# Rotary embedding on half of each head: first tile loaded in two pieces, tables from GpSimd, stores and loads regrouped

## The chip, the cores and the metric

The kernel runs on one core of one Trainium2 chip; the other cores are idle. The metric is the device time of one execution in microseconds (us). Most executions of one kernel agree within 0.3%.

## The reference

```python
batch, seq, heads, dim = (16, 512, 16, 64)          # x: float32, 33.55 MB
half_dim = dim // 2
x1, x2 = x[..., :half_dim], x[..., half_dim:]
rotated_first  = x1[..., :half_dim//2] * cos - x1[..., half_dim//2:] * sin
rotated_second = x1[..., :half_dim//2] * sin + x1[..., half_dim//2:] * cos
return concatenate([rotated_first, rotated_second, x2], axis=-1)
```

Only the first 32 values of each head's 64 are rotated; the other 32 pass through. `cos` and `sin` (512 x 32; only columns 0 to 15 are used) depend on the position alone. Every byte of `x` has to be read and every byte of the output written: 67.1 MB in all.

## The kernel before

`x` is cut into T = 4 tiles of 128 partitions x K = 16 positions ("rows"). A row is 16 heads x 64 values, 4 KiB, so that a tile is 64 KiB per partition, 8.39 MB. The kernel keeps three tiles (`NS = 3`) in SBUF, the on-chip memory that the transfers fill and empty, so tile 3 reuses tile 0's place and can be loaded only when tile 0 has been stored. VectorE rotates in place in half tiles (`KC = 8` rows), with four instructions each. All transfers are issued from one queue, that of SP, and in the trace their packets run in program order.

```python
def load(t, lo=0, hi=K):
    nc.sync.dma_start(out=rows(t, lo, hi), in_=xf[t, :, lo * R : hi * R])
def store(t, lo=0, hi=K):
    nc.sync.dma_start(out=of[t, :, lo * R : hi * R], in_=rows(t, lo, hi))

load(0)
nc.sync.dma_start(out=stage[:, 0]..., in_=cosf)      # 64 KB each
nc.sync.dma_start(out=stage[:, 1]..., in_=sinf)
load(1)
load(2)
... # 4 copies spread the tables over 128 partitions
def rotate(t, k0):
    ...
    nc.vector.tensor_mul(out=b_t[:], in0=x1, in1=s)  # b_t lies in PSUM
    nc.vector.tensor_mul(out=x1, in0=x1, in1=c)
    nc.vector.tensor_sub(...)
    nc.vector.tensor_add(...)

rotate(0, 0)
store(0, 0, KC)
rotate(0, KC)
store(0, KC, K)
load(3, 0, KC)
load(3, KC, K)
for t in range(1, T):
    rotate(t, 0)
    rotate(t, KC)
    store(t)
```

Of the kernel before, what the change touches and what calls it, by code (L numbers as in the profile page):

```python
# [1 line left out]

# [4 lines left out]


@with_exitstack
def kernel(  # L10
    ctx: ExitStack,
    tc: tile.TileContext,
    x: bass.AP,
    cos: bass.AP,
    sin: bass.AP,
    out: bass.AP,
):
    nc = tc.nc
    fp32 = mybir.dt.float32
    P = 128  # L20
    B, S, H, D = x.shape
    Q = D // 4
    HF = D // 2



    K = 16
    T = B * S // (P * K)
    PB = S // K
    REP = P // PB  # L30
    R = H * D
    NS = 3
    KC = K // 2

    xf = x.rearrange("b s h d -> (b s h d)").rearrange("(t p f) -> t p f", t=T, p=P)
    of = out.rearrange("b s h d -> (b s h d)").rearrange("(t p f) -> t p f", t=T, p=P)
    cosf = cos.rearrange("(p k) j -> p (k j)", k=K)
    sinf = sin.rearrange("(p k) j -> p (k j)", k=K)

    const_pool = ctx.enter_context(tc.tile_pool(name="const", bufs=1))  # L40
    b_pool = ctx.enter_context(tc.tile_pool(name="bp", bufs=1, space=bass.MemoryType.PSUM))


    ring = const_pool.tile([P, NS, K, H, D], fp32)
    stage = const_pool.tile([PB, 2, K, HF], fp32)
    table = const_pool.tile([P, 2, K, 2, Q], fp32)

    def rows(t, lo, hi):
        return ring[:, t % NS, lo:hi].rearrange("p k h d -> p (k h d)")

    def load(t, lo=0, hi=K):
        nc.sync.dma_start(out=rows(t, lo, hi), in_=xf[t, :, lo * R : hi * R])  # L52

    def store(t, lo=0, hi=K):
        nc.sync.dma_start(out=of[t, :, lo * R : hi * R], in_=rows(t, lo, hi))

    load(0)
    nc.sync.dma_start(out=stage[:, 0].rearrange("p k j -> p (k j)"), in_=cosf)  # L58
    nc.sync.dma_start(out=stage[:, 1].rearrange("p k j -> p (k j)"), in_=sinf)
    load(1)  # L60
    load(2)


    for r in range(REP):
        nc.vector.tensor_copy(  # L65
            out=table[r * PB : (r + 1) * PB].rearrange("p t k c j -> p (t k) c j"),
            in_=stage.rearrange("p t k j -> p (t k) j")[:, :, 0:Q]
            .unsqueeze(2)
            .to_broadcast((PB, 2 * K, 2, Q)),
        )  # L70
    C = table[:, 0].rearrange("p k c j -> p k (c j)")
    Sn = table[:, 1].rearrange("p k c j -> p k (c j)")

    def rotate(t, k0):
        x1 = ring[:, t % NS, k0 : k0 + KC, :, 0:HF]
        c = C[:, k0 : k0 + KC].unsqueeze(2).to_broadcast((P, KC, H, HF))
        s = Sn[:, k0 : k0 + KC].unsqueeze(2).to_broadcast((P, KC, H, HF))
        b_t = b_pool.tile([P, KC, H, HF], fp32)
        nc.vector.tensor_mul(out=b_t[:], in0=x1, in1=s)  # L79
        nc.vector.tensor_mul(out=x1, in0=x1, in1=c)  # L80
        nc.vector.tensor_sub(  # L81
            out=x1[:, :, :, 0:Q], in0=x1[:, :, :, 0:Q], in1=b_t[:, :, :, Q:HF]
        )
        nc.vector.tensor_add(  # L84
            out=x1[:, :, :, Q:HF], in0=x1[:, :, :, Q:HF], in1=b_t[:, :, :, 0:Q]
        )

    rotate(0, 0)
    store(0, 0, KC)
    rotate(0, KC)  # L90
    store(0, KC, K)
    load(3, 0, KC)
    load(3, KC, K)
    for t in range(1, T):
        rotate(t, 0)
        rotate(t, KC)
        store(t)


# [1 line left out]
_INS = ['x', 'cos', 'sin']  # L101
_OUTS = [((16, 512, 16, 64), 'float32')]


# [23 lines left out]
```

## Time and profile before

| | before |
|---|---|
| time, median of 3 runs | 162.21 us (162.02 to 162.35) |
| span of the profiled execution | 160.2 us |
| share of 16 DMA engines | 98.0% |
| VectorE busy | 109.5 us, 68% |
| VectorE's first instruction, end of its last | 23.9 us, 134.2 us |

The page of the profile, cut to the lines used. In part 2 each column is a fortieth of the span, about 4 us, and a digit is the busy share in tenths. Part 3 has packets, MB, and the share of 16 engines' time.

```profile
span 160.2 us, 103 instructions
## 1 busy us (share of the span) xinstructions
DVE 109.5 (68%) x36; POOL 0.2 (0%) x4
...
DVE  0000009999999999999999999999999995000000
...
GB/s 262 524 262 524 524 295 524 262 524 507 278 524 475 311 524 327 458 393 434 483 393 401 483 425 393 524 524 262 524 507 278 524 507 278 524 491 295 524 491 33
...
q1 hardware_dynamic: 1536, 67.24, 98.0%
...
DVE 61%; DMA 14%; issue 6%; DVEq 1%; SPq 0%
```

The reader should set two lines against each other. The chain that ended last (the bottom line) gives VectorE 61% and so looks like a kernel bound by VectorE. But the queue is busy 98.0% of the span. The chain follows the releaser of each *instruction*: the last store was issued when VectorE had finished, so the chain runs along VectorE. That the store then stood in a queue of other stores, this view doesn't say. The DVE row shows VectorE idle at the end, while the GB/s row goes on. (The GB/s figures swing because a 64 KiB packet is counted whole in one slice; the mean of neighbours counts.)

The timeline shows the queue of SP directly (start, duration of the issues merged, engine):

```profile
23.88 2.77 DVE L65 COPY table<-stage 32x1024 f32<-32x1024 f32 x4 [23.88 <-DMA stage<-in_sin_dram]
...
40.13 13.79 SPq L55 DMA_DIRECT2D out_dram<-ring  x2
...
72.04 10.44 SPq L52 DMA_DIRECT2D ring<-in_x_dram  x2
...
82.59 51.98 SPq L55 DMA_DIRECT2D out_dram<-ring  x3
...
131.93 2.28 DVE L84 TENSOR_TENSOR ring<-ring,b_t 128x2048 f32<-128x2048 f32 x1
```

Beside these views, the argument uses the trace's packet records (start, duration and size of each transfer on an engine). A 64 KiB packet takes 2.418 us whether it loads or stores. A completion packet of 4 bytes ends each transfer on each engine, so those packets show when the engines finished a transfer. The records don't name the engine: where this text says "per engine", a sum over all 16 is divided by 16. This gives, for three of before's five stores, when each was issued and when the first engine had nothing else to do; the difference is called the margin:

| store | issued at | engines free from | margin |
|---|---|---|---|
| tile 0, first half | 40.1 | 61.4 | 21.3 us |
| tile 2 | 107.4 | 119.6 | 12.2 us |
| tile 3, the last | 134.2 | 138.9 | 4.6 us |

The smallest margin is 4.6 us; the two stores left out have 17 us and more. While such packets run, 16 engines at 65,536 B in 2.418 us move 434 GB/s.

### The profile page before, as it was taken

The page shows a single profiled execution, that of the slowest core. Times are in us where ns is not written, and L with a number is a line of the kernel's source. Part 1 is how long each engine was busy: PE and PEld are TensorE (multiplying, and loading weights), DVE is VectorE, ACT ScalarE, POOL GpSimd, SP SyncE. Part 2 cuts the span into 40 slices and gives each one's busy share as a digit, 9 for nine tenths or more (in the row PEclk, how much of TensorE's full clock was granted, in tenths as well). Part 3 has the DMA queues.
Part 4 walks back from the last instruction along what each step waited for, and adds up shares of the span by engine and source line. Part 5 has one row for each costly group of instructions (what it writes and reads, how often), then busy time and mean ns, then how long its engine had stood idle before and what let it go on. Part 6 is the DMA issues. An engine that isn't in the chain of part 4 may idle for free.

```text
span 160.2 us, 103 instructions
## 1 busy us (share of the span) xinstructions
DVE 109.5 (68%) x36; POOL 0.2 (0%) x4
## 2 busy tenths in 40 slices
DVE  0000009999999999999999999999999995000000
POOL 0000000000000000000000000000000000000000
DMA  8969989699699797999999999996996996996990
GB/s 262 524 262 524 524 295 524 262 524 507 278 524 475 311 524 327 458 393 434 483 393 401 483 425 393 524 524 262 524 507 278 524 507 278 524 491 295 524 491 33
DMA packets 1536, 67.24 MB, mean 420 GB/s; under 512 B 192, under 2 KB 192, under 8 KB 256
## 3 DMA queue, kind: packets, MB, share of 16 engines
q1 hardware_dynamic: 1536, 67.24, 98.0%
HBM read 33.69 MB, written 33.55 MB: 420 GB/s over the span
## 4 chain that ended last, share of the span: by engine, by line
DVE 61%; DMA 14%; issue 6%; DVEq 1%; SPq 0%
DVE b_t L79 22%; DVE ring L80 22%; DMA stage<-in_sin_dram 14%; DVE ring L84 10%; DVE ring L81 6%; DVE table L65 1%; DVEq L123 1%; SPq L58 0%; SPq L52 0%; DVEq L65 0%
## 5 line engine op out<-in xcount | busy, mean ns | idle before, releaser
L79 DVE TENSOR_TENSOR b_t<-ring,table 128x4096 f32<-128x4096 f32 x8 | 35.5, 4432 | 0.3
L80 DVE TENSOR_TENSOR ring<-ring,table 128x4096 f32<-128x4096 f32 x8 | 35.4, 4424 | 0.3
L65 DVE COPY table<-stage 32x1024 f32<-32x1024 f32 x4 | 2.7, 683 | 23.9 <-DMA stage<-in_sin_dram 23.9
L81 DVE TENSOR_TENSOR ring<-ring,b_t 128x2048 f32<-128x2048 f32 x8 | 18.3, 2286 | 0.3
L84 DVE TENSOR_TENSOR ring<-ring,b_t 128x2048 f32<-128x2048 f32 x8 | 18.2, 2279 | 0.0
L112 POOL MEMSET const-bfloat16-1.0<- 128x1 bf16 x1 | 0.1, 101 | 0.0
L112 POOL MEMSET const-uint8-127<- 128x1 uint8 x1 | 0.1, 101 | 0.0
L112 POOL MEMSET const-float32-0.0<- 128x1 f32 x1 | 0.1, 98 | 0.2 <-issue 0.2
L112 POOL MEMSET const-float32-1.0<- 128x1 f32 x1 | 0.1, 98 | 0.0
## 6 DMA issues: line engine op xcount, KB each, us to landing
out_dram<-ring SPq DMA_DIRECT2D x2, 4096.0 KB, 30.2
ring<-in_x_dram SPq DMA_DIRECT2D x2, 4096.0 KB, 19.3
stage<-in_cos_dram SPq DMA_DIRECT2D x1, 64.0 KB, 22.3
stage<-in_sin_dram SPq DMA_DIRECT2D x1, 64.0 KB, 22.1
ring<-in_x_dram SPq DMA_DIRECT2D x3, 40.9
out_dram<-ring SPq DMA_DIRECT2D x3, 32.6
```

The source lines that it names most:

```text
L65: nc.vector.tensor_copy(out=table[r * PB : (r + 1) * PB].rearrange("p t k c j -> p (t k) c j"), in_=stage.rearrange("p t k j -> p (t k) j" ...
L79: nc.vector.tensor_mul(out=b_t[:], in0=x1, in1=s)
L80: nc.vector.tensor_mul(out=x1, in0=x1, in1=c)
L81: nc.vector.tensor_sub(out=x1[:, :, :, 0:Q], in0=x1[:, :, :, 0:Q], in1=b_t[:, :, :, Q:HF])
L84: nc.vector.tensor_add(out=x1[:, :, :, Q:HF], in0=x1[:, :, :, Q:HF], in1=b_t[:, :, :, 0:Q])
L112: nc = _bacc.Bacc("TRN2", target_bir_lowering=False, num_devices=1)
L123: with _tile.TileContext(nc) as tc:
```

## The change

The intent is to let VectorE start early (first 4 rows of tile 0 and the tables arrive soon), to use fewer and larger transfers (tile 0's store and tile 3's load whole), and to use the wait for that store for the second half of tile 2's load.

```diff
+    K0 = K // 4
-    load(0)
-    nc.sync.dma_start(out=stage[:, 0]..., in_=cosf)
-    nc.sync.dma_start(out=stage[:, 1]..., in_=sinf)
+    nc.gpsimd.dma_start(out=stage[:, 0]..., in_=cosf)
+    nc.gpsimd.dma_start(out=stage[:, 1]..., in_=sinf)
+    load(0, 0, K0)
+    load(0, K0, K)
     load(1)
-    load(2)
+    load(2, 0, KC)
 ... # rotate(t, k0) becomes rotate(t, lo, hi)
-    rotate(0, 0)
-    store(0, 0, KC)
-    rotate(0, KC)
-    store(0, KC, K)
-    load(3, 0, KC)
-    load(3, KC, K)
+    rotate(0, 0, K0)
+    rotate(0, K0, (K0 + K) // 2)
+    rotate(0, (K0 + K) // 2, K)
+    store(0)
+    load(2, KC, K)
+    load(3)
     for t in range(1, T):
-        rotate(t, 0)
-        rotate(t, KC)
+        rotate(t, 0, KC)
+        rotate(t, KC, K)
         store(t)
```

More of the change, by code (lines that the diff above doesn't have):

```diff
@@ L55, in store @@
         nc.sync.dma_start(out=of[t, :, lo * R : hi * R], in_=rows(t, lo, hi))
-    load(0)
-    nc.sync.dma_start(out=stage[:, 0].rearrange("p k j -> p (k j)"), in_=cosf)
-    nc.sync.dma_start(out=stage[:, 1].rearrange("p k j -> p (k j)"), in_=sinf)
+    nc.gpsimd.dma_start(out=stage[:, 0].rearrange("p k j -> p (k j)"), in_=cosf)
+    nc.gpsimd.dma_start(out=stage[:, 1].rearrange("p k j -> p (k j)"), in_=sinf)
+    load(0, 0, K0)
+    load(0, K0, K)
     load(1)
-    load(2)
+    load(2, 0, KC)
     for r in range(REP):
@@ L72, with rotate @@
     Sn = table[:, 1].rearrange("p k c j -> p k (c j)")
-    def rotate(t, k0):
-        x1 = ring[:, t % NS, k0 : k0 + KC, :, 0:HF]
-        c = C[:, k0 : k0 + KC].unsqueeze(2).to_broadcast((P, KC, H, HF))
-        s = Sn[:, k0 : k0 + KC].unsqueeze(2).to_broadcast((P, KC, H, HF))
-        b_t = b_pool.tile([P, KC, H, HF], fp32)
-        nc.vector.tensor_mul(out=b_t[:], in0=x1, in1=s)
+    def rotate(t, lo, hi):
+        n = hi - lo
+        x1 = ring[:, t % NS, lo:hi, :, 0:HF]
+        c = C[:, lo:hi].unsqueeze(2).to_broadcast((P, n, H, HF))
+        s = Sn[:, lo:hi].unsqueeze(2).to_broadcast((P, n, H, HF))
+        b_full = b_pool.tile([P, KC, H, HF], fp32, name="b_t")
+        b_t = b_full[:, 0:n]
+        nc.vector.tensor_mul(out=b_t, in0=x1, in1=s)
         nc.vector.tensor_mul(out=x1, in0=x1, in1=c)
```

## The prediction

> **What bounds the kernel now.** The DMA engines, all the time. The page gives one hardware queue at 98.0% of 16 engines' span: 67.24 MB in 160.2 us, mean 420 GB/s. VectorE is busy 68%, so the chain of waits (DVE 61%) misleads: in the timeline VectorE is done at 134.2 us, and the store queued behind it ends at 158.8. In the trace's packet records a 64 KiB packet takes 2.418 us, a 32 KiB packet 1.213 us, loads and stores alike. 16 engines at 65,536 B / 2.418 us are 434 GB/s. The Trainium skill ("DMA: Bandwidth & Descriptors", section "Where 436 GB/s comes from") puts the ceiling at 435.2 GB/s; this trace agrees: nothing is left in the rate.
>
> The span adds up (estimate from these records): first packet at 1.74 us; 67.1 MB are 64 packets per engine x 2.418 = 154.8; the very first packets take about 3.3 us, +0.85; the tables plus the slow packet after them (2.9 us) cost about 0.75; the tail after the last packet is 1.4. Sum 159.5 of 160.2. Between first and last packet the engines are practically never idle.
>
> **What the change does.** Bytes and arithmetic stay. It
> - starts VectorE earlier: it now waits 23.9 us for the second table, which queues behind all of tile 0. After: the first 4 rows land at 8-9 us, the tables in 5-14. The table copies take 2.8 us, 4 rows half of 13.45. Rows 4-16 still land at about 22.5, so tile 0 is finished at about 43 us; before, its second half was at 53.6.
> - stores tile 0 whole at 43, not in halves at 40.1 and 53.6. All of these precede the end of the queued loads: load 1 ends at 42, the half load of tile 2 at 51.5. The store follows with no gap (margin 8 us).
> - puts the rest of load 2 behind that store: 71 to 80.6 us. Load 3 is issued when store 0 has landed (about 72.5), 8 us before the queue runs dry. Load 3 runs to 100, store 1 to 119, store 2 to 139, store 3 to 158.
> - loads tile 3 whole: VectorE ends at about 128.5, 10 us before store 3 may start.
>
> In neither kernel does a stage starve the queue, and VectorE's gain lies wholly off the critical path. What remains: the tables leave SP's queue. The skill's same page ("Issuing engines are not separate DMA queues") says that GpSimd's DMAs run on the same 16 engines, so their 128 KB still cost about 0.35 us; the slowed packets after them (0.4 us) may go. GpSimd's issue may cost a little; the run before can't show that.
>
> **Prediction.** 161.9 us (162.2 less 0.3), range 161.1 to 162.9. Faster by over 2%: 0.01; within 2%: 0.97; slower by over 2%: 0.02.
>
> **What the profile would show.** Right: DMA share of both queues together about 98%, GB/s slices of 393-430 in the mean throughout; first table copy at 6-15 us; VectorE's idle time split up, with waits for tile 0's rest (a few us) and load 3 (about 4); VectorE busy still 109.5 us; store 0 issued at 42-45 us, load 3 at about 72, span 159.5-160.7. Wrong: a gap of DMA slices near 51, 81 or 139 us; 64 KiB packets over 2.42 us beside GpSimd's queue; a later first load.
>
> **What would make it wrong.** Tables landing after 21 us, starved by large packets: then tile 0 is done after 51 us and the queue stands still until then. A fixed cost of GpSimd's DMA at start or end, of 1 us or more. Imbalance among the engines.

## The result, and the profile after

After takes 161.93 us (161.85 to 162.03, 6 runs); before took 162.07 us (161.90 to 162.35, 6 runs, three of them those quoted above). The ratio is 0.9991, with a 95% interval of 0.9978 to 1.0003: the same, and the 0.14 us between the medians aren't clear of noise. (Ratios in this text are the mean time of one kernel's runs over that of the other's of the same rounds, so not quite the ratio of the medians.)

The page of after, the lines that answer to those of before. There are two queues now, q0 being GpSimd's:

```profile
span 160.1 us, 109 instructions
## 1 busy us (share of the span) xinstructions
DVE 110.0 (69%) x40; POOL 1.3 (1%) x6
...
DVE  0069709999999999999999994799999900000000
...
GB/s 197 385 504 454 393 459 524 262 524 491 295 401 581 328 524 409 377 393 418 483 540 295 491 524 262 524 524 262 524 524 262 524 524 262 524 491 295 524 459 66
...
q1 hardware_dynamic: 1440, 67.11, 97.8%
q0 software_dynamic: 64, 0.13, 0.2%
...
DMA 50%; DVE 28%; DVEq 1%; issue 0%; SPq 0%
```

VectorE's row begins four columns further left and ends two columns further left. The DMA share of both queues together is 98.0%, to the digit that of before. The chain has turned from DVE 61% into DMA 50% with no change of the time: it describes which instruction released which, and isn't a measure of what a microsecond is worth.

The timeline of after:

```profile
9.13 2.77 DVE L67 COPY table<-stage 32x1024 f32<-32x1024 f32 x4 [9.13 <-DMA stage<-in_sin_dram]
...
23.66 3.37 DVE L83 TENSOR_TENSOR b_t<-ring,table 128x3072 f32<-128x3072 f32 x1 [4.71 <-DMA ring<-in_x_dram]
...
44.14 0.35 SPq L56 DMA_DIRECT2D out_dram<-ring  x1
...
44.53 28.14 SPq L53 DMA_DIRECT2D ring<-in_x_dram  x2
...
72.77 55.64 SPq L56 DMA_DIRECT2D out_dram<-ring  x3
...
101.19 4.43 DVE L83 TENSOR_TENSOR b_t<-ring,table 128x4096 f32<-128x4096 f32 x1 [3.29 <-DMA ring<-in_x_dram]
...
125.77 2.28 DVE L88 TENSOR_TENSOR ring<-ring,b_t 128x2048 f32<-128x2048 f32 x1
```

VectorE starts 14.8 us earlier (9.13 against 23.88) and ends 6.2 us earlier (128.05 against 134.21); most of the rest it lost by waiting for rows 4 to 15 of tile 0 (4.71 us) and for tile 3 (3.29 us). The end of the program didn't move with it: the engines' last packet ends at 158.60 us, before it was 158.79. The margins of the stores now are:

| store | issued at | engines free from | margin |
|---|---|---|---|
| tile 0 | 44.1 | 51.7 | 7.6 us |
| tile 2 | 97.9 | 119.4 | 21.5 us |
| tile 3, the last | 128.1 | 138.7 | 10.7 us |

So the change moved margin about: from the head (21.3 to 7.6 us) to the end (4.6 to 10.7). Margin isn't time: in neither kernel was there a gap in the transfers that an earlier store could have closed.

### The profile page after: what moved, and what is told of

Its sections match the earlier page's. It is cut to its first block, busy times and chain, and to the rows that moved or that the text cites. A ratio compares the mean times of both kernels' runs of the same rounds, so it can differ in the third digit from the quotient of the medians.

```text
span 160.1 us, 109 instructions
## 1 busy us (share of the span) xinstructions
DVE 110.0 (69%) x40; POOL 1.3 (1%) x6
## 4 chain that ended last, share of the span: by engine, by line
DMA 50%; DVE 28%; DVEq 1%; issue 0%; SPq 0%
DMA ring<-in_x_dram 32%; DMA out_dram<-ring 18%; DVE b_t L83 10%; DVE ring L84 10%; DVE ring L85 5%; DVE ring L88 3%; DVEq L127 1%; SPq L53 0%; DVEq L83 0%
## 5 line engine op out<-in xcount | busy, mean ns | idle before, releaser
L83 DVE TENSOR_TENSOR b_t<-ring,table 128x4096 f32<-128x4096 f32 (+2 forms) x9 | 35.6, 3959 | 8.2 <-DMA ring<-in_x_dram 8.0
L84 DVE TENSOR_TENSOR ring<-ring,table 128x4096 f32<-128x4096 f32 (+2 forms) x9 | 35.6, 3950 | 0.3
L85 DVE TENSOR_TENSOR ring<-ring,b_t 128x2048 f32<-128x2048 f32 (+2 forms) x9 | 18.4, 2049 | 0.3
L88 DVE TENSOR_TENSOR ring<-ring,b_t 128x2048 f32<-128x2048 f32 (+2 forms) x9 | 18.4, 2042 | 0.0
L58 POOL DMA_DIRECT2D stage<-in_cos_dram x1 | 0.6, 631 | 0.8 <-PEq L127 0.8
L59 POOL DMA_DIRECT2D stage<-in_sin_dram x1 | 0.5, 498 | 0.0
```

The source lines that it names most:

```text
L58: nc.gpsimd.dma_start(out=stage[:, 0].rearrange("p k j -> p (k j)"), in_=cosf)
L59: nc.gpsimd.dma_start(out=stage[:, 1].rearrange("p k j -> p (k j)"), in_=sinf)
L83: nc.vector.tensor_mul(out=b_t, in0=x1, in1=s)
L85: nc.vector.tensor_sub(out=x1[:, :, :, 0:Q], in0=x1[:, :, :, 0:Q], in1=b_t[:, :, :, Q:HF])
L88: nc.vector.tensor_add(out=x1[:, :, :, Q:HF], in0=x1[:, :, :, Q:HF], in1=b_t[:, :, :, 0:Q])
```

## The experiments

My theory: the DMA engines bound both kernels at their full rate, without a gap; VectorE matters only where it is later than its margin over the queue. Rivals: VectorE's chain is (part of) the time; VectorE's traffic slows the transfers; GpSimd's queue saves or costs something; loads and stores together can go beyond 434 GB/s.

### No rotation at all

```diff
 # after, without the rotations (the result is wrong on purpose)
-    rotate(0, ...)   # three calls
-        rotate(t, 0, KC)
-        rotate(t, KC, K)
```

> Kernel after without any rotation (wrong result on purpose): VectorE only builds the tables, each store waits for its load alone. Theory (VectorE is wholly off the critical path, and does not slow the DMA engines): 161.7 to 162.0, 64 KiB packets still 2.418 us. Rival A (the chain of waits is right, VectorE's 28% of it is on the path): shorter by 10 us or more. Rival B (VectorE's SBUF traffic slows the packets): shorter by 1 us or more, shorter packets.

Measured: 162.03 us (161.83 to 162.28, 4 runs), ratio to before 1.0000 (0.9986 to 1.0013). Lines of its page:

```profile
span 160.0 us, 65 instructions
...
DVE 2.7 (2%) x4; POOL 1.3 (1%) x6
...
q1 hardware_dynamic: 1440, 67.11, 97.7%
```

Some 107 us of VectorE work are worth nothing, and the packets are no shorter. Both rivals about VectorE fall, and nothing is left of VectorE's 61% (or 28%) of the chain.

### The parts of the change that concern the tables

Three runs. The first is before with the tables alone moved to GpSimd:

```diff
-    load(0)
-    nc.sync.dma_start(out=stage[:, 0]..., in_=cosf)   # and sin
+    nc.gpsimd.dma_start(out=stage[:, 0]..., in_=cosf) # and sin
+    load(0)
```

> Kernel before with one part of the change alone: the two table loads issued from GpSimd, ahead of load 0. Theory (the DMA engines are busy without a gap, tables cost engine time wherever they are issued): within 0.2 us of before (about 161.9 to 162.1), table packets still take about 0.33 us per engine. Rival A (leaving SP's queue removes a drain of 0.4 us that the tables cause): 161.6 or less. Rival B (a fixed cost of GpSimd's DMA at the start or end): above 162.5. VectorE's first rotation still waits for tile 0, at about 23 us.

Measured: 162.06 us (161.92 to 162.44, 5 runs), ratio 1.0004 (0.9991 to 1.0017). Neither rival. VectorE's table copies start at 16.5 us there, later than in after (9.1); the likely reason is that beside GpSimd's packets SP's queue now has packets of 64 KiB instead of 16 KiB. The first rotation starts at 23.8 us, about as expected. Beside GpSimd's packets, between 7 and 16 us, the 64 KiB packets took 2.52 to 2.78 us instead of 2.42, about 0.5 us per engine in all. The prediction had listed such a slowing as a sign against itself; the time doesn't show it.

The second is after with the tables put back on SP's queue:

```diff
-    nc.gpsimd.dma_start(out=stage[:, 0]..., in_=cosf) # and sin
     load(0, 0, K0)
+    nc.sync.dma_start(out=stage[:, 0]..., in_=cosf)   # and sin
     load(0, K0, K)
```

> Kernel after with the tables put back on SP's queue, between the first 4 rows and the next 12. Theory (bytes through the engines are all that counts): 161.9 to 162.2, no difference from after or before that clears 0.2%; first table copy at about 9 us as with GpSimd. Rival (GpSimd's queue is what gave the 0.14 us between the two medians): 162.1 or more, with slowed packets right after the tables.

Measured: 162.01 us (161.70 to 162.18, 5 runs), ratio to before 0.9996 (0.9983 to 1.0008). The table copies start at 8.77 us, even a little before after's 9.13. The slowed packets of the rival are there as well: behind the tables the 48 KiB packets took 2.06 to 2.10 us instead of 1.82, 0.25 us per engine, which the time doesn't show. So VectorE's early start doesn't come from GpSimd but from the cut of tile 0 into 4 and 12 rows, with the tables behind the 4.

The third is before without any loading of tables:

```diff
-    nc.sync.dma_start(out=stage[:, 0]..., in_=cosf)   # and sin
+    nc.vector.memset(stage[:], 0.5)                   # wrong result on purpose
```

> Kernel before without the two table loads; VectorE fills the tables with 0.5 (wrong result on purpose). It measures what the tables cost. My sum in the prediction said 0.75 us (0.35 for bytes, 0.4 for the slowed packet behind them): then about 161.3. If only the bytes cost: about 161.7. If the tables hid in something else: 162.1.

Measured: 161.92 us (161.74 to 162.01, 5 runs), ratio 0.9990 (0.9976 to 1.0003): about 0.14 us, not the 0.75 of my sum, and not clear of nothing. The packet records of the one profiled execution show how: load 1 ends 0.9 us earlier than in before (its last completion packet at 41.6 against 42.5 us), as the sum said. But the last packets of load 2, just before the first store, took 1.2 us per engine longer than usual, where before had 0.02. By the end of load 2 the lead was gone (62.2 against 61.9). So in this profile a saving of 0.9 us early in the queue was given back at the first change from loading to storing.

### How much VectorE may be late

To measure the margins, VectorE was given more work: the first multiplication of one piece is repeated, which changes no result.

```diff
-        nc.vector.tensor_mul(out=b_t, in0=x1, in1=s)
+        for _ in range(1 + extra):
+            nc.vector.tensor_mul(out=b_t, in0=x1, in1=s)
-    rotate(0, 0)                                # in before
+    rotate(0, 0, extra=2)                       # b_extra2; 3 in b_extra3; 4.43 us each
-    rotate(0, K0, (K0 + K) // 2)                # in after
+    rotate(0, K0, (K0 + K) // 2, extra=1)       # a_extra1; 2 and 4 in the others; 3.37 us each
```

> Kernel before with VectorE made late: the first multiplication of tile 0's first half is done three times instead of once, 8.9 us more of VectorE work (result unchanged). Theory (a late VectorE costs only what exceeds its margin over the DMA queue): the tightest margin of before is the last store, issued at 134.2 us while the engines finish store 2 from 138.9 on. With 8.9 us more it is issued at 143.1, its first packet comes about 1 us later, 5.2 us after the engines ran dry: about 167.3 us. Rival A (VectorE's chain is the time): 171.0. Rival B (nothing VectorE does matters): 162.1.

> As b_extra2 with three extra multiplications, 13.3 us. Theory: last store issued at 147.5, first packet 9.6 us after the engines ran dry: about 171.7 us. Rival A: 175.4. Rival B: 162.1.

> Kernel after with two extra multiplications (3.37 us each, 6.7 us) in tile 0's second piece. Theory: the tightest margin is now store 0, issued at 44.1 us, while the engines finish the queued loads from 51.7 on. It is issued at 50.9, its first packet at about 51.9: still about 162.0, at most 162.5. Rival A: 168.7.

> Kernel after with four extra multiplications, 13.5 us, as much as b_extra3 has. Theory: store 0 is issued at 57.6, first packet about 6.9 us after the engines ran dry: about 168.8 us, 3 us less than b_extra3, and the gap in the DMA slices lies near 52 to 58 us instead of near 140 to 148. Rival A: 175.4. Rival B: 162.

| kernel | VectorE's extra | expected | measured | ratio to before (95%) |
|---|---|---|---|---|
| b_extra2 | 8.9 us | 167.3 | 166.79 | 1.0287 (1.0270 to 1.0304) |
| b_extra3 | 13.3 us | 171.7 | 171.07 | 1.0559 (1.0539 to 1.0579) |
| a_extra2 | 6.7 us | 162.0 to 162.5 | 163.87 | 1.0104 (1.0082 to 1.0126) |
| a_extra4 | 13.5 us | 168.8 | 170.39 | 1.0510 (1.0492 to 1.0528) |

The two of before came out within 0.7 us of the theory, and both rivals are over 4 us off. In b_extra3 tile 2's store is late as well (13.3 us of extra work against its margin of 12.2), which the expectation had overlooked: the packet records have one hole from 119.4 to 121.5 us and one from 140.9 to 148.4, together the 9.6 us that were expected in one piece. In b_extra2 the last store is issued at 143.52 us (timeline), after the engines ran dry, and the stretch before its first packets is empty (the last two columns are DMA share and GB/s):

```profile
143.52 0.33 SPq L55 DMA_DIRECT2D out_dram<-ring  x1
```

```profile
139.80:144.30 4.50, 3.69 (x2) 0.00 (x0) 1.00 0.00 0
```

In a_extra4 the hole is where the theory put it, before the first store (row of its page, 4.2 us a column; the column with 8 GB/s begins at 50.6 us):

```profile
GB/s 191 525 373 373 560 498 249 498 498 365 381 490 8 249 342 404 498 498 249 373 607 264 498 498 482 264 404 342 498 498 404 342 498 498 389 358 498 498 389 109
```

But for after the theory missed: a_extra2 was to take 162.5 us at most and took 163.87, and a_extra4 took 1.6 more than expected. In a_extra2 store 0 is issued at 50.86 us, before the engines are free at 51.6. Its page shows engines as busy as ever, since a slowed packet counts as busy for as long as it lasts:

```profile
span 161.8 us, 111 instructions
...
q1 hardware_dynamic: 1440, 67.11, 97.7%
```

There is no hole, but some packets were longer. At two changes of direction the last packet on each engine, usually 2.42 us, took 2.9 to 3.9: at 69 to 72 us (store 0 to load 2) and at 98 to 102 us (load 3 to store 1). With the first packets behind them it makes 1.7 us per engine. In after the same two changes cost 0.1 us. a_extra4 has them too, 2.0 us together. That accounts for what was missed: without the 1.6 and 1.9 us that these two have more than after, they would stand at 162.3 and 168.5, where the theory had 162.0 to 162.5 and 168.8.

Two more runs asked when these slow packets come. In a_extra_t1 the extra work lies in tile 1:

```diff
-        rotate(t, 0, KC)
+        rotate(t, 0, KC, extra=2 if t == 1 else 0)
```

> a_extra2 came out 1.9 us slower than after, where the theory allowed 0.5: its engines had no gap, but the last packets before two changes of direction (store 0 to load 2b near 70 us, load 3 to store 1 near 100 us) were slow, 0.7 and 0.9 us per engine. This is the same with one extra multiplication, 3.4 us: store 0 is issued at about 47.5 us, 4 us before the queue has finished. If slow packets come only when store 0 reaches the queue about when it runs dry (in a_extra2 0.9 us before): 161.9 to 162.1, no slow packets at 70 and 100. If any later VectorE costs: about 163.

> Kernel after with 8.9 us more of VectorE work in tile 1 instead of tile 0: store 0 is issued at 44.1 as in after, but VectorE is later from there on, and is busy near 98 us where in after it waits for load 3 (as it is busy there in a_extra2). If the slow packets of a_extra2 come from the late issue of store 0: 161.9 to 162.1. If they come from VectorE working during the change from load 3 to store 1: about 162.9, slow packets near 98 alone. Margin of the last store: VectorE ends at about 133.7, the engines need it from 138.7 on, so no gap.

Measured: a_extra1 162.32 us (162.02 to 162.68, 6 runs), ratio to before 1.0007 (0.9981 to 1.0033); a_extra_t1 162.53 us (162.22 to 162.65, 5 runs), ratio 1.0019 (0.9994 to 1.0045). (One of the 11 runs of before beside them took 163.22 us, which widens the intervals; the medians lie 0.3 and 0.5 us above before's 162.01.) So store 0 may be 3.4 us later, and VectorE 8.9 us later from tile 1 on, at a cost that isn't clear of nothing and is at most 0.5%. Both medians fell between the two times that were expected (161.9 to 162.1, or about 163), so the times decide neither question. The extra time per engine at the changes of direction, from the packet records of one execution each:

| kernel | store 0 issued, us before the engines are free | last load before store 0 | store 0 to load 2 (in before: to load 3) | last load before store 1 |
|---|---|---|---|---|
| before | 21.3 | 0.02 | 0.04 | 0.03 |
| b_no_tables | 25.4 | 1.18 | 0.00 | 0.04 |
| b_gp_tables | 24.3 | 0.35 | 0.00 | 0.06 |
| after | 7.6 | 0.06 | 0.04 | 0.05 |
| a_no_rotate | 28.1 | 0.06 | 0.02 | 0.07 |
| a_sp_tables | 8.2 | 0.53 | 0.00 | 0.08 |
| a_extra_t1 | 7.6 | 0.00 | 0.05 | 0.00 |
| a_extra1 | 4.5 | 0.37 | 0.00 | 0.50 |
| a_extra2 | 0.7 | 0.02 | 0.83 | 0.89 |
| a_extra4 | late by 6.0 | 0.06 | 0.83 | 1.17 |

(b_extra2 and b_extra3 are not in the table; their changes of direction cost at most 0.1 us each.) In the one profiled execution of a_extra_t1 VectorE is busy near 98 us and there is no slow packet, so being busy there isn't enough to cause one. But that execution was the fastest of its five (162.22 us; the others took 162.44 to 162.65), and the one of a_extra1 was the slowest of its six (162.68); what the others did at these changes isn't known. The late issue of store 0 goes along with the slow packets in the last two lines. But it can't be the only condition, since b_no_tables has the slowest of all at the first change with 25 us to spare. What decides whether a change of direction is free or costs 1 us stays open.

### Loads and stores on two queues

```diff
 def store(t, lo=0, hi=K):
-    nc.sync.dma_start(out=of[t, :, lo * R : hi * R], in_=rows(t, lo, hi))
+    nc.scalar.dma_start(out=of[t, :, lo * R : hi * R], in_=rows(t, lo, hi))
```

> Kernel after with the stores on ScalarE's DMA queue, the loads left on SP's, so that loads and stores that are ready at the same time share the engines. It tests whether 434 GB/s is the engines' rate in any mixture, and whether the order of the one queue matters. Theory (the rate belongs to the engine): from 44 to 80 us, where loads 1, 2 and store 0 overlap, still 430 GB/s or less. Store 0 lands later, at about 81 us, so load 3 is issued later, shares with store 1, lands at about 120 us, VectorE ends at about 147: a gap in the DMA slices before the last store, about 170 us. Rival (loads and stores use two directions that can run at once): above 480 GB/s in the overlap and a time under 160.

Measured: 180.52 us (180.42 to 180.74, 4 runs), ratio 1.1110 (1.1044 to 1.1177). Stretches of its span, the last two columns being DMA share and GB/s; below them the waits of VectorE:

```profile
44.00:80.00 36.00, 35.72 (x11) 0.00 (x0) 1.00 1.01 428
80.00:139.00 59.00, 25.98 (x8) 0.00 (x0) 1.00 1.00 432
139.00:158.00 19.00, 18.00 (x7) 0.00 (x0) 1.00 0.00 0
158.00:178.00 20.00, 0.00 (x0) 0.00 (x0) 1.00 0.97 419
```

```profile
DVE b_t L83 <- DMA ring<-in_x_dram: 37.6, 3, 25.3
```

From 44 to 139 us, where loads and stores share the engines until the last load ends at 129.8, they move 428 and 432 GB/s, no more than one direction at a time. The rival falls: 434 GB/s is the most for both directions together. Whether the engines, the memory or what lies between them sets it, no run here separates. The loss is one of order. Sharing with the stores, tile 3's load ends at 129.8 us (in after at 100.6), VectorE waits 25.3 us for it, and the engines stand still for 19 us before the last store. I had expected 170, because I had counted only store 1 beside load 3; the second half of load 2 was delayed as well (to 91.1 us, in after 81.3), and the start of load 3 behind it. The Trainium skill suggests this split ("Perfetto Trace Analysis", section "DMA Optimizations", to put inputs on one issuing engine and outputs on another "to allow more dynamic spread", above all with loops or control flow, which this kernel has not); here the one queue in a good order was better by 18.5 us. Its "DMA: Bandwidth & Descriptors", section "Queues, rings and completion order", says that an engine takes turns between queues packet by packet; this trace agrees: from 46 to 60 us the packet records have 64 packets of each queue, and as those of the load were of 32 KiB and those of the store of 64, the load got a third of the bytes.

### Could fewer bytes be moved?

Half of each head isn't changed. If it could be left out of the transfers, the bound would fall. The last store, only the rotated half, in runs of 128 bytes:

```diff
-        store(t)                                 # for t = 3
+    nc.sync.dma_start(
+        out=of[T - 1].rearrange("p (n d) -> p n d", d=D)[:, :, 0:HF],
+        in_=ring[:, (T - 1) % NS].rearrange("p k h d -> p (k h) d")[:, :, 0:HF],
+    )
```

> Kernel after whose last store writes only the rotated half of each head, in runs of 128 bytes (wrong result on purpose: the other half of tile 3 isn't written). It asks whether the pass-through half could be left out of the transfers. If time went by bytes, the last store takes 9.7 instead of 19.3 us: 152.3. Theory (a descriptor per run costs more than its bytes): from the trace, 2 KiB packets of the tables took 84 ns where the rate alone gives 76, so about 8 ns on top: 2048 runs per engine of 4.7 + 8 ns are 26 us, time about 168.5; more if short writes cost extra, up to 200.

Measured: 166.85 us (one look, state unknown; before took 162.01 beside it). The stretch of the last store, and the page:

```profile
139.50:163.30 23.80, 0.00 (x0) 0.00 (x0) 1.00 1.61 175
```

```profile
DMA packets 34144, 63.05 MB, mean 382 GB/s; under 512 B 32960, under 2 KB 32960, under 8 KB 32992
```

(A share of 1.61 can't be a share of time: the records of these short packets overlap.) Half the bytes take 24.3 us (138.98 to 163.25 in the packet records) where the whole store takes 19.3. That is 11.9 ns per run on each engine (24.3 us for 2,048 runs), 173 GB/s in all; the estimate had been 12.7 ns. So this way down is closed for stores: half a tile in such runs costs more than the whole tile in one piece. Loads in such runs, or a copy from DRAM to DRAM of the half that passes through, were not tried.

## Why the prediction was right

- **What bounds it** (right). The share of 98.0% stayed to the digit; without any rotation the time is the same; in a mixture of directions the rate doesn't rise. The ceiling of 435.2 GB/s that the Trainium skill states ("DMA: Bandwidth & Descriptors", section "Where 436 GB/s comes from") agrees with the 434 of the packets.
- **VectorE's gain is off the critical path** (right). It starts 14.8 us and ends 6.2 us earlier, and the time moves by 0.14 us. Its first copy came at 9.13 us (6 to 15 predicted), its waits were 4.71 and 3.29 us ("a few" and "about 4").
- **No gap at 51, 81 or 139 us** (right). Store 0 was issued at 44.1 us (42 to 45), load 3 at about 72.3 (72), the span was 160.1 (159.5 to 160.7). The margin of store 0 was 7.6 us (8), that of the last store 10.7 (10).
- **The tables' small gain** (size wrong, within the range). I put tables and the slow packet behind them at 0.75 us and hoped for 0.3 of it. This step of the prediction, that the slow packets may go, failed: in after they only changed place: 16 KiB packets beside GpSimd's took up to 0.95 instead of 0.61 us, together with the next of 48 KiB about 0.6 us per engine, as much as the one slow 64 KiB packet behind the tables before (0.5). Taking the tables away altogether gave 0.14 us with an interval that includes 0. The median of 161.93 beside my 161.9 is therefore not evidence for that step.
- **VectorE busy still 109.5 us** (off by 0.5): 110.0, with four more instructions.
- **What I hadn't seen**: that a full queue isn't quite the whole story. A margin of 7.6 us can't be spent to the last microsecond: 6.7 us of extra work cost 1.7 (163.87 against 162.19 for before in the same rounds), in slower packets at changes of direction, not in a hole.

No version was faster than both kernels by more than the noise. Without any arithmetic, without tables, or with the tables' part of the change alone or left out, the median stays between 161.9 and 162.1 us. (The cut of tile 0 and the regrouped transfers were not run one by one.) Of the 160.1 us span of after, 154.9 are packets at the usual duration of their size; the rest is the start until the first packet (1.75), the tail after the last (1.5), slow first packets (0.65), slow packets beside the tables (0.6), the tables and completion packets (0.45) and changes of direction (0.3).

## What to carry to other kernels

Before moving work forward, ask what the queue is doing at the moment when the work ends: if the transfer that it releases would only stand behind others, the gain is margin and not time. The chain of waits can name an engine that could be removed altogether without a change; here the share of the DMA queue together with the last packet's end named the limit, and the run without arithmetic confirmed it. And on a full queue the order of the transfers matters: one queue in a good order took 162 us, two queues with the same transfers 180.

## What the Trainium skill lacked or had wrong

- "DMA: Bandwidth & Descriptors": it names no cost for a change between loading and storing. Here the packets around such a change, mostly the last ones before it, cost from 0 to 1.2 us per engine beyond the usual (0.02 in before, 1.18 in b_no_tables, 0.89 and 1.17 at one change in a_extra2 and a_extra4). The condition is not settled.
- The same page gives a completion latency for a single DMA but says nothing about slow neighbours of small transfers: after the tables' 2 KiB packets the next 64 KiB packet took up to 3.0 instead of 2.42 us, and beside GpSimd's 4 KiB packets those of 16 KiB took up to 0.95 instead of 0.61.
- The same page warns of descriptors under 512 B, but its only rates for stores to HBM in runs of 128 bytes are for another chip than this one. Here it was 11.9 ns per run and engine, about 173 GB/s.
- "Perfetto Trace Analysis", section "DMA Optimizations": separate issuing engines for inputs and outputs are advised without the caution that the loads then share the engines with stores that nobody waits for. Here it cost 11% (180.5 against 162.0 us).
